# Rotary embedding from PSUM on VectorE, and stabiliser rows loaded in four parts, in a hybrid mLSTM and window-attention layer

## The chip, the cores and the metric

The kernel runs on 1 core of one Trainium2 chip. The metric is the device time of one launch in microseconds (us). The engines are TensorE (PE, with PEld for its weight loads), VectorE (DVE), ScalarE (ACT), GpSimd (POOL) and SyncE (SP), which issues nearly all DMAs.

## The reference

One layer of a diffusion backbone, in float32: 1024 latent tokens and 256 context tokens of width 1024. The tokens are normalised and modulated, and one projection `u = h @ w_in` gives the inputs of two groups of heads:

```
q_m, k_m = silu(dwconv3(qk))          # mLSTM, 4 heads x 128, both directions, stabilised by running maxima
q_a, k_a, v_a                         # window attention, 8 query heads and 2 key heads x 64
y_a = window_attention(rope(q_a) * 64**-0.5, rope(k_a), v_a, k_ctx, v_ctx, sink)
rope: y0 = x0*cos - x1*sin ; y1 = x0*sin + x1*cos      # x0, x1: 16 columns each, twice in a head of 64
x = x + g_a * (concat(y_m, y_a) @ w_out)
x = x + g_f * conv_glu(modulate(rmsnorm(x)))
```

The mLSTM decays are exp(d - m), and the rows of m (the stabilisers) are needed along the free dimension of a tile, the same in all partitions.

## The kernel before

All large products split each operand into a high and a low half that TensorE takes at its fast rate, and sum three products. The work goes in this order:

1. **Norm and shared projection** (to about 78 us of the span). Tokens are normalised, transposed and modulated; `px_mm` projects block c (128 tokens) onto gates, keys and values of the attention, and `px_out(c)` takes the result out of PSUM: VectorE adds the gate biases (L321), ScalarE copies the values into the tile `kv` (L326), which has 3 buffers, and `kv` is stored to DRAM by SP. Keys of latent blocks (c from 2 on) are rotated in between: a ScalarE copy to `kr`, two GpSimd products with the cosine and sine tables (`ta`), a GpSimd subtraction and a GpSimd addition. The blocks 6 and 7 lie in the two banks of one PSUM tile (`pa`), whose slot the first product of `dense` (tile `pp`, L583) takes next. The order of PE, DVE, ACT and POOL is written out by hand here.
2. **Head 0's projection** (`dense(0)`), where a planner orders all engines, and the chain of gate arithmetic (`gate_chain`), which ends with the rows of m in the DRAM tensor `m_d`.
3. **Four mLSTM heads** (about 128 to 376 us). `mlstm(h)` is a generator; each of its 30 steps is followed by products of `dense(h+1)` or, in the last head, of the query projection (`qgen`), so that TensorE has other work. Beside it, `ada_second` streams the rest of `w_ada` in 64 pieces of 256 KB (tile `w2`, 2 buffers: piece i issues the load of piece i+2) and multiplies and adds them on VectorE (L812, L814). At a head's start `ee` (8 blocks, 1 buffer) is loaded from `m_d`, broadcast to all partitions, in one DMA of 1 MB (L641); `mask(b)` adds the triangle on VectorE (L654), `decay(b)` takes the two exponentials on ScalarE (L658), and `first` multiplies with the scores (L714). In the first loop of 9 steps, which carries the backward state (L679, L681), step i does `mask(i-1)`. In the heads 0 to 2 the order of all engines and of SP's DMAs is the program's; in head 3 only PE's is, and the planner orders the others.
4. **Query projection, to about 413 us**: 16 times 24 matmuls into PSUM (`px`, 2 buffers), then the rotation into `z`, the split into `qs` (`qtrans`: ScalarE L865, VectorE L866), a transpose on TensorE (L870) and a store to `q_d`. The transposes of one step are emitted some steps later (`LAG`). Three tiles of `w_out` are multiplied by a gate row, on VectorE, GpSimd and VectorE (`load_wo`, L878).
5. **Attention with the output projection** (to about 600 us), all engines ordered by the planner; then the ConvGLU and the down projection, which take the rest of the span.

Of the kernel before, what the change touches and what calls it, by code (L numbers as in the profile page):

```python
# [8 lines left out]
F32 = mybir.dt.float32  # L9
F32R = mybir.dt.float32r  # L10
BF16 = mybir.dt.bfloat16
AF = mybir.ActivationFunctionType
ALU = mybir.AluOpType
# [4 lines left out]
P = 128  # L18
# [55 lines left out]
def build(tc, I, out, dbg=None):  # L74
# [229 lines left out]

    pxs = {}

    def px_mm(c, kts):
        if c not in pxs:
            if c in (6, 7):

                pxs[c] = pas[-1][:, 512 * (c - 6):512 * (c - 6) + 512]
            else:
                pool, tag = (pl, "l") if c >= 2 else (pd, "d")
                pxs[c] = pool.tile([P, 512], F32, name="px", tag=tag)
        px = pxs[c]
        for kt in kts:
            mm3(px[:, :XW], hsl(0, kt, c), hsl(1, kt, c), wX[0][:, kt, :], wX[1][:, kt, :], kt == K0[0], kt == K1[-1])

    def px_out(c):
        px = pxs.pop(c)  # L320
        V.tensor_tensor(out=gates[:, c, :], in0=px[:, 0:16], in1=rwc("gate_b"), op=ALU.add)  # L321
        kv = xp.tile([P, 2 * P], F32, name="kv", tag="kv", bufs=3)
        if c < NC:
            S.copy(kv[:], px[:, 16:XW])
        else:
            S.copy(kv[:, P:], px[:, 16 + P:XW])  # L326
            kr = xp.tile([P, P], F32, name="kr", tag="kr")
            S.copy(kr[:], px[:, 16:16 + P])  # L328
            ta = xp.tile([P, 2, P], F32, name="ta", tag="ta", bufs=1)
            for i in range(2):  # L330
                G.tensor_tensor(out=ta[:, i].rearrange("p (h e) -> p h e", h=KVH),
                                in0=kr[:].rearrange("p (h e) -> p h e", h=KVH),
                                in1=rope[:, i, c - NC].unsqueeze(1).broadcast_to([P, KVH, ADH]), op=ALU.mult)
            tv = ta[:].rearrange("p i (a s j) -> p i a s j", s=2, j=16)
            kvv = kv[:, :P].rearrange("p (a s j) -> p a s j", s=2, j=16)
            G.tensor_tensor(out=kvv[:, :, 0], in0=tv[:, 0, :, 0], in1=tv[:, 1, :, 1], op=ALU.subtract)
            G.tensor_tensor(out=kvv[:, :, 1], in0=tv[:, 1, :, 0], in1=tv[:, 0, :, 1], op=ALU.add)
        nc.sync.dma_start(kv_d[c], kv[:])

    K0, K1 = (1, 3, 0, 2), (5, 7, 4, 6)  # L340
# [289 lines left out]
    def mlstm(h, kT, qT, va):  # L630
# [7 lines left out]


        ee = tp.tile([P, NL, 2, P], F32, name="ee", tag="ee", bufs=1)  # L640
        nc.sync.dma_start(ee[:], m_d[:].rearrange("(c h) d t -> h c d t", h=H)[h:h + 1, NC:].broadcast_to([P, NL, 2, P]))  # L641
        def tr(c):
            pn = pl.tile([P, 512], F32, name="pn", tag="l")
            T.transpose(pn[:, 0:P], kT[:, c * P:(c + 1) * P], ident[:])
# [8 lines left out]
        def mask(b):  # L653
            V.tensor_tensor(out=ee[:, b], in0=ee[:, b], in1=tri[:], op=ALU.add)  # L654
# [10 lines left out]
        for i, c in enumerate(order[1][:-1]):  # L665
            pn, kwb = ahead.pop(0)
            if i + 2 < NCH - 1:
                ahead.append(tr(order[1][i + 2]))
            elif i + 2 == NCH - 1:
                tr(order[1][i + 2])  # L670
            T.matmul(pn[:, P:P + E1], kwb[:], va[:, c], start=True, stop=True)
            if c == 1:
                nx = tp.tile([P, E1], F32, name="cst", tag="cst")[:]
            elif c == 0:
                nx = cbk[:, NL - 1]
            else:
                nx = cbk[:, c - NC - 1]
            if prev is None:
                V.tensor_copy(nx, pn[:, P:P + E1])  # L679
            else:  # L680
                V.scalar_tensor_tensor(out=nx, in0=prev, scalar=g1(gd, 1, c), in1=pn[:, P:P + E1],  # L681
                                       op0=ALU.mult, op1=ALU.add)
            prev = nx
            if fins and i:
                next(fins[0])
            if i:
                mask(i - 1)
            if i and i % 2 == 0:
                decay(i // 2 - 1)
            if i == TN:  # L690

                S.activation(yv, yv, AF.Tanh, scale=0.5)
                V.scalar_tensor_tensor(out=yv, in0=yv, scalar=1.0, in1=rwc("gain", h * DH, DH).unsqueeze(1)
                                       .broadcast_to([P, NL, DH]), op0=ALU.add, op1=ALU.mult)
            yield
# [48 lines left out]
        for c in range(NC):  # L744
            pn = pl.tile([P, 512], F32, name="pn", tag="l")
            step(c, pn[:, 0:E1])
            if c == 0:
                cfs.clear()
            decay(4 + c)
            yield  # L750
        first(NC)
        tail = None
# [1 line left out]
        for c in range(NC, NCH):  # L754
            if c + 1 < NCH:
                first(c + 1)
            if tail:
                next(tail)
            yield
            if c < NC + 2:  # L760
                decay(6 + c - NC)
            if tail:
                next(tail)
            tail = second(c)
            yield
# [75 lines left out]
    def qproj(i, b):  # L841
# [5 lines left out]
                yield 0.64  # L847
        if i == 0:
            zs.append(pq.tile([P, 2, 2 * P], F32, name="z", tag="p_", bufs=PB, padded_shape=[P, 2, 320]))
        qt = zs[b][:, i]  # L850
        S.activation(qt, px[:, :256], AF.Copy, scale=float(ADH) ** -0.5)  # L851
        ta = xp.tile([P, 2 * P], F32, name="ta3", tag="ta", bufs=1)
        q4 = qt.rearrange("p (h e) -> p h e", h=4)
        rp_ = lambda j: rope[:, j, b].unsqueeze(1).broadcast_to([P, 4, ADH])
        G.tensor_tensor(out=ta[:].rearrange("p (h e) -> p h e", h=4), in0=q4, in1=rp_(1), op=ALU.mult)  # L855
        V.tensor_tensor(out=q4, in0=q4, in1=rp_(0), op=ALU.mult)
        tv = ta[:].rearrange("p (a s j) -> p a s j", s=2, j=16)
        qv = qt.rearrange("p (a s j) -> p a s j", s=2, j=16)
        G.tensor_tensor(out=qv[:, :, 0], in0=qv[:, :, 0], in1=tv[:, :, 1], op=ALU.subtract)
        G.tensor_tensor(out=qv[:, :, 1], in0=qv[:, :, 1], in1=tv[:, :, 0], op=ALU.add)  # L860

    def qtrans(i, b):
        qs = pq.tile([P, 4, 2, ADH], F32R, name="qs", tag="qs", bufs=3)
        qh = zs[b][:, i].rearrange("p (h e) -> p h e", h=4)
        S.copy(qs[:, :, 0], qh)  # L865
        V.tensor_tensor(out=qs[:, :, 1], in0=qh, in1=qs[:, :, 0].bitcast(F32), op=ALU.subtract)  # L866
        yield
        pt = pl.tile([P, 512], F32, name="pt", tag="l")
        for j in range(4):
# [75 lines left out]
    for h in range(H):  # L945
# [20 lines left out]
        with tc.manual_schedule(engines=order_):  # L966
            dn = dense(h + 1, wkq, wvo, *nh) if nh else qgen()
            rate = RATE if nh else RATE3
            for n, _ in enumerate(mlstm(h, *cur)):
# [9 lines left out]
                elif nh and n in (24, 27):  # L979
                    wkq = wnext((n // 27,))  # L980
                    if n == 27 and h + 2 < H:
                        wnext = ahead_load(h + 2, 1)
                elif nh and n % 8 != 7:
                    next(ada, 0)
                debt += rate * (1 + (n == 0))
                while debt > 0:
# [178 lines left out]
            V.tensor_tensor(out=yf[0:64], in0=u[0:64, 0:P], in1=ut[0:64], op=ALU.add)  # L1165
            V.tensor_tensor(out=yf[64:128], in0=u[64:128, P:2 * P], in1=ut[64:128], op=ALU.add)

    wos += [load_wo(k, (G, V)[k % 2], lw, "w4") for k in range(1, 4)]
    w0 = wout_m(0)
    next(w0)  # L1170
    for g in qpend:
# [795 lines left out]
def host_pack(inp):  # L1967
# [55 lines left out]
    inv = (10000.0 ** (-np.arange(16, dtype=np.float32) / 16)).astype(np.float32)  # L2023
    ang = np.stack([(t // 64).astype(np.float32)[:, None] * inv, (t % 64).astype(np.float32)[:, None] * inv], 1)
    tab = np.stack([np.cos(ang), np.sin(ang)], 0).astype(np.float32)
    tab = np.repeat(tab[:, :, :, None, :], 2, 3).reshape(2, NL, P, ADH)
    r["rope"] = np.ascontiguousarray(tab.transpose(2, 0, 1, 3))
    return r

# [17 lines left out]
```

## Time and profile before

| | us |
|---|---|
| median of 3 runs | 1310.68 (1309.24 to 1312.76) |
| profiled execution, its own time | 1308.92 |
| span of its trace | 1306.9 |
| time around the span | 2.0 |
| TensorE busy in the span | 1255.5 |
| VectorE busy | 980.7 |
| ScalarE busy | 635.3 |
| GpSimd busy | 253.1 |

The times of the rows below are from the profiled execution, in us from the start of its span. A busy TensorE is not one at its peak, and a granted clock below 1.00 makes its matmuls longer.

### The profile page before, as it was taken

How to read it: one execution, taken by the hardware profiler on the slowest of the kernel's cores; microseconds unless marked ns; L12 is line 12 of the kernel's file. 1: busy time of each engine (PE TensorE's matmuls, PEld its weight loads, DVE VectorE, ACT ScalarE, POOL GpSimd, SP SyncE). 2: the span in 40 equal slices, each digit the busy share in tenths (PEclk: the TensorE clock that was granted, in tenths of full speed). 3: DMA queues.
4: the chain of work that ended last, by engine and by line, in shares of the span. 5: the costliest groups of instructions: out<-in, count | busy, mean ns of one | idle time of the engine just before them, and what ended most of it. 6: DMA issues, size and time to landing. Idle time of an engine off the chain costs nothing.

```text
span 1306.9 us, 19479 instructions
## 1 busy us (share of the span) xinstructions
PE 1255.5 (96%) x7071; PEld 1068.6 (82%) x7071; DVE 980.7 (75%) x1752; ACT 635.3 (49%) x1295; POOL 253.1 (19%) x252
## 2 busy tenths in 40 slices
PE   6999999999898999999989999999999999999997
PEld 4789998989898777878768788888888888788886
DVE  5754777777665888897898777777777776867887
ACT  6632546464764666776664333333333333434435
POOL 1240000000134223332411222222212222001000
PEclk9999999999998999999989999999999999999999
DMA  9431535362245322211422333322322326975653
GB/s 362 169 117 35 156 116 149 106 174 73 66 144 179 113 66 97 78 69 64 147 97 97 105 105 105 112 99 105 104 97 105 105 105 235 340 283 165 202 199 130
DMA packets 90226, 175.64 MB, mean 134 GB/s; under 512 B 12746, under 2 KB 29330, under 8 KB 90130
## 3 DMA queue, kind: packets, MB, share of 16 engines
q1 hardware_dynamic: 89842, 173.61, 39.7%
q8 instruction: 56, 0.92, 0.3%
q10 hardware_dynamic: 288, 0.79, 0.2%
q14 instruction: 40, 0.33, 0.1%
HBM read 136.04 MB, written 38.33 MB: 133 GB/s over the span
## 4 chain that ended last, share of the span: by engine, by line
PE 53%; DVE 8%; ACT 3%; DMA 2%; issue 2%; POOL 1%; SPq 0%; ACTq 0%; DVEq 0%; POOLq 0%
PE pd L1892 14%; PE pc L1384 8%; PE pa L1384 8%; PE pe L1384 4%; PE pb L1384 4%; PE pd L1384 4%; PE u L1154 2%; PE po L301 2%; PE po L303 2%; PE po L302 1%; DVE nm L1102 1%; PE pt L1131 1%; DMA ar<-act_s 1%; DVE nm L1103 1%; PE pf L1384 0%
## 5 line engine op out<-in xcount | busy, mean ns | idle before, releaser
L1486 ACT CAST wh<-Rb 128x1024 fp32r<-128x1024 f32 (+1 forms) x66 | 59.5, 904 | 144.6 <-PE pd L1384 81.6
L1892 PE MATMUL pd<-dh,al 128*128 128x512 f32 x296 | 115.5, 390 | 0.8 <-DVE al L1258 0.8
L1892 PE MATMUL pd<-dl,ah 128*128 128x512 f32 x296 | 115.4, 390 | 0.0
L1892 PE MATMUL pd<-dh,ah 128*128 128x512 f32 x296 | 115.3, 389 | 0.0
L1384 PE MATMUL pc<-hB,wh 128*128 128x512 f32 x344 | 106.5, 391 | 1.1 <-DVE av L1463 1.1
L1384 PE MATMUL pa<-hB,wh 128*128 128x512 f32 x336 | 103.7, 390 | 0.0
L1274 DVE TENSOR_TENSOR wl<-Rb,wh 128x1024 fp32r<-128x1024 f32 (+1 forms) x66 | 68.9, 1046 | 39.4 <-ACT wh L1486 38.8
L1594 POOL TENSOR_TENSOR tt<-vt,tt 128x512 f32<-128x512 f32 x22 | 29.5, 1341 | 321.5 <-ACT tt L1588 321.5
L583 PE MATMUL pp<-hl,wh 128*128 128x512 f32 x256 | 79.4, 406 | 1.3 <-ACT kr L328 1.3
L1384 PEld LDWEIGHTS pc<-hB,wh 128*128 128x128 f32 x344 | 64.8, 189 | 15.0 <-DVE av L1463 1.6
L301 PE MATMUL pv<-wh,hl 128*128 128x256 f32 x256 | 76.0, 297 | 0.0
L1384 PEld LDWEIGHTS pa<-hB,wh 128*128 128x128 f32 x336 | 63.0, 188 | 13.4 <-ACT sn L1558 0.4
L303 PE MATMUL pv<-wh,hl 128*128 128x256 f32 x256 | 72.4, 283 | 0.0
L302 PE MATMUL pv<-wl,hl 128*128 128x256 f32 x256 | 72.4, 283 | 0.0
L855 POOL TENSOR_TENSOR ta<-z,rope 128x256 f32<-128x256 f32 x16 | 13.4, 838 | 285.4 <-ACT z L851 285.4
L1384 PE MATMUL pc<-hB,wl 128*128 128x512 f32 x172 | 67.0, 389 | 0.0
L1892 PEld LDWEIGHTS pd<-dh,al 128*128 128x128 f32 x296 | 55.6, 188 | 12.9 <-DVE al L1258 1.5
L1384 PE MATMUL pa<-hB,wl 128*128 128x512 f32 x168 | 65.4, 389 | 0.0
L1892 PEld LDWEIGHTS pd<-dl,ah 128*128 128x128 f32 x296 | 55.6, 188 | 11.9 <-DVE dl L1258 0.3
L1892 PEld LDWEIGHTS pd<-dh,ah 128*128 128x128 f32 x296 | 55.6, 188 | 11.5
L1138 ACT CAST ph<-pt 128x512 fp32r<-128x512 f32 (+1 forms) x88 | 45.3, 526 | 21.8 <-PE pt L1131 21.3
L1102 DVE TENSOR_REDUCE nm<-sps 128x1 f32<-128x640 f32 (+1 forms) x64 | 50.0, 783 | 6.3 <-PE sps L1098 5.7
(1078 smaller groups left out, 3836.4 us busy)
## 6 DMA issues: line engine op xcount, KB each, us to landing
w<-in_w_ada_dram SPq DMA_DIRECT2D x64, 256.0 KB, 2.7
br<-in_w_down_dram SPq DMA_DIRECT2D x25, 512.0 KB, 6.3
Ra<-in_w_up_dram SPq DMA_DIRECT2D x22, 512.0 KB, 3.6
Rb<-in_w_up_dram SPq DMA_DIRECT2D x22, 512.0 KB, 3.6
ar<-act_s SPq DMA_DIRECT2D x44, 256.0 KB, 3.1
act_a<-tt SPq DMA_DIRECT2D x33, 256.0 KB, 2.0
act_s<-tt SPq DMA_DIRECT2D x33, 256.0 KB, 2.0
wr<-in_w_h_dram SPq DMA_DIRECT2D x16, 512.0 KB, 4.4
```

The source lines that it names most:

```text
L301: T.matmul(ps, st_hi, mv_hi, start=first, stop=False)
L302: T.matmul(ps, st_hi, mv_lo, start=False, stop=False)
L303: T.matmul(ps, st_lo, mv_hi, start=False, stop=last)
L583: T.matmul(pp[:, 512 * n:512 * n + 512], wkq[sw][:, kt, cs], hl[n][part][:, kt, :], start=kt == 0 and sw + part == 0, stop=kt == KT - 1 an ...
L1102: V.tensor_reduce(out=self.nm[:, j:j + 1], in_=self.sv[j], axis=AX.X, op=ALU.max, negate=True)
L1138: S.copy(self.ph[i][:, :w], self.pt[i][:, :w])
L1154: T.matmul(self.u[:], vv[:, c, self.g], part[i][:, kk * 2 * P:(kk + 1) * 2 * P], start=kb + m == 0, stop=kb == last and m == 1)
L1274: sub = lambda e, o, x, y: e.tensor_tensor(out=o, in0=x, in1=y, op=ALU.subtract)
L1384: T.matmul(ps[:], wt[sw][:, j, ks], hB[part][:, blk, kt, :], start=first and kt == 0 and sw + part == 0, stop=last and kt == 3 and sw == 1 ...
L1486: S.copy(wt[0][:], src)
L1594: G.tensor_tensor(out=self.tt[:, h2_], in0=self.vt[:], in1=self.tt[:, h2_], op=ALU.mult)
L1892: T.matmul(ps[:], ac[sa][:, js], w[sw], start=first and n == 0, stop=last and n == 2, skip_group_check=not fresh)
```

## The change

Four edits. **Rotation**: keys and queries are rotated by three VectorE operations, the two products reading PSUM, the third an addition in place whose second input has each pair of 16-column groups swapped; the sine table on the host gets the sign. The ScalarE copies `kr` and `z` are gone, and the scale of 1/8 goes into the split in `qtrans`. **Rows**: `ee` is loaded in four DMAs of two blocks, one at the head's start and one in each of the steps i = 0, 1, 2; `mask` and `decay` come a step or two later. **Pieces of `w_ada`**: no longer in the steps n = 0 and 1 of a head, but in n = 7 and 23. **`w_out`**: all three gate products on VectorE.

```
+    def rotate(dst, src, nh, b):
+        ta = xp.tile([P, nh * ADH], F32, name="ta", tag="ta", bufs=1)
+        hv = lambda a: a.rearrange("p (h e) -> p h e", h=nh)
+        sv = lambda a: a.rearrange("p (a s j) -> p a s j", s=2, j=16)
+        for i, o in ((1, ta[:]), (0, dst)):
+            V.tensor_tensor(out=hv(o), in0=hv(src), in1=rope[:, i, b].unsqueeze(1).broadcast_to([P, nh, ADH]), op=ALU.mult)
+        V.tensor_tensor(out=sv(dst), in0=sv(dst), in1=sv(ta[:])[:, :, ::-1], op=ALU.add)
...
             S.copy(kv[:, P:], px[:, 16 + P:XW])
-            kr = xp.tile([P, P], F32, name="kr", tag="kr")
-            S.copy(kr[:], px[:, 16:16 + P])
-            ta = xp.tile([P, 2, P], F32, name="ta", tag="ta", bufs=1)
-            for i in range(2):
-                G.tensor_tensor(out=ta[:, i].rearrange("p (h e) -> p h e", h=KVH),
...
-            G.tensor_tensor(out=kvv[:, :, 0], in0=tv[:, 0, :, 0], in1=tv[:, 1, :, 1], op=ALU.subtract)
-            G.tensor_tensor(out=kvv[:, :, 1], in0=tv[:, 1, :, 0], in1=tv[:, 0, :, 1], op=ALU.add)
+            rotate(kv[:, :P], px[:, 16:16 + P], KVH, c - NC)
...
-        nc.sync.dma_start(ee[:], m_d[:].rearrange("(c h) d t -> h c d t", h=H)[h:h + 1, NC:].broadcast_to([P, NL, 2, P]))
+        def ee_load(b):
+            nc.sync.dma_start(ee[:, b:b + 2], m_d[:].rearrange("(c h) d t -> h c d t", h=H)
+                              [h:h + 1, NC + b:NC + b + 2].broadcast_to([P, 2, 2, P]))
+
+        ee_load(0)
...
             prev = nx
+            if i < 3:
+                ee_load(2 * i + 2)
             if fins and i:
                 next(fins[0])
-            if i:
-                mask(i - 1)
-            if i and i % 2 == 0:
-                decay(i // 2 - 1)
+            if i > 1:
+                mask(i - 2)
+            if i in (4, 6, 8):
+                decay(i // 2 - 2)
...
-            decay(4 + c)
+            if c == 0:
+                mask(NL - 1)
+            decay(3 + c)
...
-            if c < NC + 2:
-                decay(6 + c - NC)
+            if c < NC + 3:
+                decay(5 + c - NC)
...
-        qt = zs[b][:, i]
-        S.activation(qt, px[:, :256], AF.Copy, scale=float(ADH) ** -0.5)
-        ta = xp.tile([P, 2 * P], F32, name="ta3", tag="ta", bufs=1)
...
-        G.tensor_tensor(out=ta[:].rearrange("p (h e) -> p h e", h=4), in0=q4, in1=rp_(1), op=ALU.mult)
-        V.tensor_tensor(out=q4, in0=q4, in1=rp_(0), op=ALU.mult)
...
-        G.tensor_tensor(out=qv[:, :, 0], in0=qv[:, :, 0], in1=tv[:, :, 1], op=ALU.subtract)
-        G.tensor_tensor(out=qv[:, :, 1], in0=qv[:, :, 1], in1=tv[:, :, 0], op=ALU.add)
+        rotate(zs[b][:, i], px[:, :256], 4, b)
...
-        S.copy(qs[:, :, 0], qh)
-        V.tensor_tensor(out=qs[:, :, 1], in0=qh, in1=qs[:, :, 0].bitcast(F32), op=ALU.subtract)
+        S.activation(qs[:, :, 0], qh, AF.Copy, scale=float(ADH) ** -0.5)
+        V.scalar_tensor_tensor(out=qs[:, :, 1], in0=qh, scalar=float(ADH) ** -0.5, in1=qs[:, :, 0].bitcast(F32),
+                               op0=ALU.mult, op1=ALU.subtract)
...
-                elif nh and n % 8 != 7:
+                elif nh and n >= 3 and n != 15:
                     next(ada, 0)
...
-    wos += [load_wo(k, (G, V)[k % 2], lw, "w4") for k in range(1, 4)]
+    wos += [load_wo(k, V, lw, "w4") for k in range(1, 4)]
...
-    tab = np.repeat(tab[:, :, :, None, :], 2, 3).reshape(2, NL, P, ADH)
+    tab = np.repeat(tab[:, :, :, None, :], 2, 3)
+    tab[1, :, :, 1] *= -1
+    tab = tab.reshape(2, NL, P, ADH)
```

## Rows read from the trace of the kernel before

**Rows 1.** The page's first part: busy us of each engine in the span, its share, and the number of instructions.

```profile
PE 1255.5 (96%) x7071; PEld 1068.6 (82%) x7071; DVE 980.7 (75%) x1752; ACT 635.3 (49%) x1295; POOL 253.1 (19%) x252
```

**Rows 2.** Busy time of each engine in stretches of the span. Columns: the stretch and its length, then busy us (and instructions) of PE, PEld, DVE, ACT and POOL, the granted clock of TensorE, the DMA share and GB/s.

```profile
62.00:90.00 28.00, 25.39 (x161) 22.86 (x160) 14.52 (x41) 10.56 (x25) 18.28 (x34) 1.00 0.40 113
128.00:200.00 72.00, 72.00 (x518) 67.18 (x517) 49.29 (x115) 36.19 (x109) 0.00 (x0) 1.00 0.46 136
200.00:265.00 65.00, 63.73 (x460) 59.21 (x459) 49.27 (x121) 34.97 (x99) 0.00 (x0) 1.00 0.42 127
330.00:375.00 45.00, 39.64 (x316) 37.85 (x315) 31.45 (x106) 33.70 (x106) 8.78 (x15) 0.96 0.24 72
375.00:425.00 50.00, 45.63 (x360) 42.72 (x358) 29.80 (x60) 25.86 (x62) 23.12 (x36) 0.93 0.62 190
450.00:560.00 110.00, 104.84 (x719) 86.44 (x720) 97.52 (x243) 76.49 (x199) 38.81 (x43) 1.00 0.24 82
```

**Rows 3.** The waits of TensorE between 60 and 450 us: who waited, for whom, us in total, how many times, the longest.

```profile
PE pn L644 <- DVE cst L679: 2.4, 2, 1.2
PE pn L644 <- DVE cbk L681: 2.1, 1, 2.1
PE pn L671 <- ACT kwf L650: 1.6, 3, 1.2
PE pt L870 <- DVE qs L866: 1.5, 3, 0.9
PE pa L303 <- DVE hl L297: 1.3, 2, 0.7
PE pp L583 <- ACT kr L328: 1.3, 1, 1.3
PE pt L870 <- DVE nm L1103: 1.2, 1, 1.2
...
PE pt L870 <- ACT QTo L872: 0.9, 1, 0.9
```

**Rows 4.** The timeline of VectorE in the heads 1, 2 and 3 of the mLSTM: start, length, the instruction, and in brackets the idle time before it and what ended it.

```profile
204.95 0.49 DVE L812 TENSOR_SCALAR acc<-w,scc 128x512 f32<-128x512 f32 x1 [6.83 <-DMA w<-in_w_ada_dram]
205.35 0.28 DVE L679 COPY cst<-pn 128x129 f32<-128x129 f32 x1
...
274.23 0.75 DVE L814 SCALAR_TENSOR_TENSOR acc<-w,scc,acc 128x512 f32<-128x512 f32 x1 [6.50 <-DMA w<-in_w_ada_dram]
...
341.85 0.76 DVE L654 TENSOR_TENSOR ee<-ee,tri 128x256 f32<-128x256 f32 x2 [3.08 <-DMA ee<-m_d]
342.52 0.34 DVE L681 SCALAR_TENSOR_TENSOR cbk<-cbk,gd,pn 128x129 f32<-128x129 f32 x1
```

**Rows 5.** The instructions on the tile `ee`: line, engine, operation, count, shortest, median and longest ns, the first and last start, and the shape; and the time of its loads from issue to landing.

```profile
L654 DVE TENSOR_TENSOR ee<-ee,tri x32: 374/420/428, 139.7 to 348.2; 128x256 f32<-128x256 f32 x32
L714 DVE SCALAR_TENSOR_TENSOR ee<-pe,ee x32: 409/417/425, 158.2 to 368.2; 128x256 f32<-128x256 f32 x32
L641 SPq DMA_DIRECT2D ee<-m_d x4: 366/372/382, 130.3 to 333.7; - x4
...
DMA to landing us min/median/max: 8.1/9.3/9.8
```

**Rows 6.** DMA issues: tile and source, queue, count, KB each, median us from issue to landing.

```profile
w<-in_w_ada_dram SPq DMA_DIRECT2D x64, 256.0 KB, 2.7
```

**Rows 7.** The instructions of the rotation, in the form of rows 5: those on the tile `ta`, the ScalarE copy, and VectorE's product in the last 50 us of the stage.

```profile
L331 POOL TENSOR_TENSOR ta<-kr,rope x16: 454/463/1478, 61.9 to 84.4; 128x128 f32<-128x128 f32 x16
L855 POOL TENSOR_TENSOR ta<-z,rope x16: 728/740/1761, 344.8 to 413.3; 128x256 f32<-128x256 f32 x16
L859 POOL TENSOR_TENSOR z<-z,ta x16: 454/460/578, 347.5 to 414.6; 128x128 f32<-128x128 f32 x16
...
L851 ACT ACTIVATE z<-px x16: 365/377/387, 344.3 to 412.8; 128x256 f32<-128x256 f32 x16
...
L856 DVE TENSOR_TENSOR z<-z,rope x11: 411/425/426, 378.7 to 414.1; 128x256 f32<-128x256 f32 x11
```

**Rows 8.** The timeline of VectorE and ScalarE around the blocks of keys and values.

```profile
61.17 0.17 DVE L321 TENSOR_TENSOR gates<-px,rw 128x16 f32<-128x16 f32 x1
61.38 0.27 ACT L326 COPY kv<-px 128x128 f32<-128x128 f32 x1 [0.84 <-DVE gates L321]
64.24 0.70 DVE L297 TENSOR_TENSOR hl<-ym,hl 128x512 fp32r<-128x512 f32 x1 [2.90 <-POOL ym L292]
...
77.91 0.27 ACT L326 COPY kv<-pa 128x128 f32<-128x128 f32 x1 [5.12 <-DMA kv_d<-kv]
```

**Rows 9.** The timeline of GpSimd and VectorE where GpSimd multiplies a tile of `w_out`.

```profile
398.74 2.39 POOL L878 TENSOR_TENSOR wor<-wor,rga 128x1024 f32<-128x1024 f32 x1
...
399.25 2.16 DVE L866 TENSOR_TENSOR qs<-z,qs 128x256 fp32r<-128x256 f32 x1 [1.09 <-ACT qs L865]
```

**Rows 10.** The stretches of 4 us in which TensorE's granted clock fell, between 300 and 450 us; columns as in rows 2.

```profile
344.00:348.00 4.00, 3.55 (x16) 3.25 (x17) 4.00 (x14) 3.43 (x14) 1.19 (x2) 0.57 0.22 82
416.00:420.00 4.00, 2.98 (x10) 2.04 (x11) 4.00 (x8) 3.56 (x6) 0.00 (x0) 0.51 0.90 247
420.00:424.00 4.00, 4.00 (x19) 3.22 (x18) 1.00 (x6) 0.87 (x3) 1.35 (x2) 0.64 0.75 282
```

**Rows 11.** The instructions of the tile `wor` on VectorE, in the form of rows 5.

```profile
L878 DVE TENSOR_TENSOR wor<-wor,rga x3: 1215/1217/1226, 389.0 to 424.8; 128x1024 f32<-128x1024 f32 x3
```

More of the change, by code (lines that the diff above doesn't have):

```diff
@@ L326, in px_out @@
             S.copy(kv[:, P:], px[:, 16 + P:XW])
-            kr = xp.tile([P, P], F32, name="kr", tag="kr")
-            S.copy(kr[:], px[:, 16:16 + P])
-            ta = xp.tile([P, 2, P], F32, name="ta", tag="ta", bufs=1)
-            for i in range(2):
-                G.tensor_tensor(out=ta[:, i].rearrange("p (h e) -> p h e", h=KVH),
[L332 to L335, printed above, removed]
-            G.tensor_tensor(out=kvv[:, :, 0], in0=tv[:, 0, :, 0], in1=tv[:, 1, :, 1], op=ALU.subtract)
-            G.tensor_tensor(out=kvv[:, :, 1], in0=tv[:, 1, :, 0], in1=tv[:, 0, :, 1], op=ALU.add)
+            rotate(kv[:, :P], px[:, 16:16 + P], KVH, c - NC)
         nc.sync.dma_start(kv_d[c], kv[:])
@@ L849, in qproj @@
             zs.append(pq.tile([P, 2, 2 * P], F32, name="z", tag="p_", bufs=PB, padded_shape=[P, 2, 320]))
-        qt = zs[b][:, i]
-        S.activation(qt, px[:, :256], AF.Copy, scale=float(ADH) ** -0.5)
-        ta = xp.tile([P, 2 * P], F32, name="ta3", tag="ta", bufs=1)
-        q4 = qt.rearrange("p (h e) -> p h e", h=4)
-        rp_ = lambda j: rope[:, j, b].unsqueeze(1).broadcast_to([P, 4, ADH])
-        G.tensor_tensor(out=ta[:].rearrange("p (h e) -> p h e", h=4), in0=q4, in1=rp_(1), op=ALU.mult)
-        V.tensor_tensor(out=q4, in0=q4, in1=rp_(0), op=ALU.mult)
-        tv = ta[:].rearrange("p (a s j) -> p a s j", s=2, j=16)
-        qv = qt.rearrange("p (a s j) -> p a s j", s=2, j=16)
-        G.tensor_tensor(out=qv[:, :, 0], in0=qv[:, :, 0], in1=tv[:, :, 1], op=ALU.subtract)
-        G.tensor_tensor(out=qv[:, :, 1], in0=qv[:, :, 1], in1=tv[:, :, 0], op=ALU.add)
+        rotate(zs[b][:, i], px[:, :256], 4, b)
     def qtrans(i, b):
```

## The prediction

> **What bounds the kernel now.** I read the page's first part, then the busy time by stage, then TensorE's own waits, then the timeline at each wait. The reader should see that TensorE is busy 96% of the span [rows 1], so another engine's work counts only where TensorE waits for it, or where its clock falls. It stands idle 2.6 us among the keys and values (62 to 90 us), not at all in head 0 (128 to 200), 1.3 us in head 1 (200 to 265), but 5.4 and 4.4 us in the two stretches from 330 to 425 us [rows 2]. The list of TensorE's waits names the causes, and most touch the edits: the backward state (L679, L681, 2.4 and 2.1 us), a copy in head 3 (L650), the splits of queries (L866, 1.5), keys and modulated tokens (L328, L297), and the last two query steps (0.9 and 1.2) [rows 3]. The clock falls twice, each time right after such waits: to a mean of 0.57 in 344 to 348 us and of 0.51 and 0.64 in 416 to 424 us, that is to its lower level of 1.2 GHz for part of each [rows 10]. A mean of 0.57 over 4 us costs (1 - 0.57) x 4 = 1.7 us of full-speed work, the second fall 1.96 + 1.44 = 3.4 us.
>
> **The change part by part.**
>
> *Keys.* GpSimd's order puts two modulating products behind the rotation of block 2, and VectorE stands 2.90 us waiting for them [rows 8]; TensorE loses 1.3 us there [rows 3]. With GpSimd free these products can run before, so that I give back all 1.3. The other wait, 1.3 us before `pp`, is for block 7's copies: ScalarE's copy into `kv` stood 5.12 us because an earlier store of `kv` had not landed [rows 8]. The stores now follow a shorter chain, so this wait should shrink, but SP has other loads in front of them; I take half, 0.7. VectorE's price: a 128x256 operation on PSUM takes 417 ns [rows 5] and a 128x16 one 170 [rows 8]; on the line between them 128x128 is about 0.285 us (an estimate). Eight blocks by three are 6.8 us more on an engine busy 14.5 of 28 [rows 2], so 76%. One thing speaks against it. ScalarE's copy starts at 61.38, 40 ns after the gate addition on the same PSUM tile ends (61.17 + 0.17) [rows 8]: the two engines read a tile one after the other. So the rotation must wait for that copy, and VectorE, in order, stands wherever the copy waits for a store; behind it are the next gates, the splits of head 0's weights and the gate chain. If the store lands no earlier than now, `pp` opens after one copy and two products (0.27 + 0.57) and not after two copies (0.54 at most): 0.3 later, with a change of engine up to 0.5, whatever was gained ahead of it. Keys: **2.0 us**, from -0.5 to 2.6. The Trainium skill has this as a rule ("PSUM — Partial Sum Buffer", section "PSUM bank collisions raise a hardware error"): two engines must not read one bank at a time, reads against reads included. By that rule, the trace agrees, the low bound is the case in which a store is late.
>
> *Heads 1 and 2.* VectorE stands 6.83 and 6.50 us for a 256 KB piece of `w_ada` in the step before L679 [rows 4]. Such pieces land in 2.7 us [rows 6]; these were issued behind the 1 MB of `ee`, which takes 8.1 to 9.8 [rows 5]. L679 behind them keeps TensorE from its next slot, 1.2 us each [rows 3]. Now no piece stands in steps 0 and 1, and only 256 KB of rows go first; the pieces of step 3 were issued in the head before. The later parts of `ee` are issued in steps 2 to 4 between pieces, in SP's written order, and each is first read four steps later (about 2 us a step, 30 steps in 65 us [rows 2]), against 2.7 us for a load of that size. SP issues 3 more DMAs of 0.37 us a head [rows 5], on a queue that waits more than it works. The pieces in steps 7 and 23 are 0.75 us of VectorE work each [rows 4], under TensorE's filler products. **2.4 us**, from 0 to 2.4. Head 0 has no idle TensorE [rows 2] and gains nothing. Masks and decays keep count and length; what moves still comes steps ahead of L714, so 0.
>
> *Head 3.* VectorE's first mask waits 3.08 us for the whole of `ee`, L681 stands behind it [rows 4], TensorE waits 2.11 us, then 1.19 us more for a copy that ScalarE does after the delayed exponentials [rows 3], and then runs 4 us at a mean clock of 0.57. A quarter of the load should land in some 3 us and not in 8 to 9, before the first mask now needs it, and each mask is a step later. 2.11 + 1.19 + 1.7 = **5.0 us**; if only half of the waits go and the clock still falls, 1.6. A rule of the Trainium skill speaks against parts ("DMA: Bandwidth & Descriptors", section "Bandwidth": batch transfers to at least 1 MiB). By the rows four loads of 256 KB one after the other are 4 x 2.7 = 10.8 us against 9.3 [rows 5, 6], so the last part comes 1.5 us later than the whole does now, the first 6.6 earlier. By that rule the last masks would be the late ones, which is a rival below.
>
> *Queries.* A step's chain was ScalarE 0.38, GpSimd 0.74, VectorE 0.43, GpSimd 2 x 0.46, then the split [rows 7]; now three VectorE operations of about 0.42 in a row, 1.26 against 2.47 plus four changes of engine. No row has the reversed groups of 16 on VectorE: below, 0.417 as for L714 [rows 5]; above, GpSimd's own price for the strided form against the dense one, 2 x 0.46 against 0.74, which is 1.24 times, so 0.52. I take 0.42, since only strides differ. The one long split, 2.16 us for 0.42, ran beside GpSimd's 2.39 us product on `w_out` [rows 9], which now takes 1.22 on VectorE [rows 11]. So the 1.5 us behind L866 should go (0.6 if the longest, 0.9, stays away and the rest remains gone only in part): **1.5 us**. At the end, 0.9 us waited for a ScalarE copy that stood behind a split waiting for GpSimd, and 1.2 for the last query's chain, which is now more than 1.2 us shorter: **2.1 us**, at least 0.5. The clock's second fall comes right behind; whether it goes I leave open, 0 to 3.4, taking 0, because the fall's work would then partly wait for the splits of `w_out`.
>
> *New cost.* In 375 to 425 us VectorE is busy 29.8 of 50 [rows 2]; 11 query steps [rows 7] x 2 more operations x 0.42 are 9.2, the product on `w_out` 1.2: 40.2 of 50. That hides behind TensorE's 24 matmuls a step, unless a 1.22 us operation stands in front of a rotation whose PSUM buffer is wanted. I charge one, **-1.3 us** with its hand-over; at most three, -3.7; at least 0.
>
> Sum: 2.0 + 2.4 + 5.0 + 1.5 + 2.1 - 1.3 = 11.7 us. The profiled execution took 1308.92, so 1297.2; it lies 1.76 under the median of the runs, so against 1310.68 the forecast is **1299.0**.
>
> **The rivals.**
>
> (a) *The parts arrive late.* The third and fourth quarter, queued behind pieces of `w_ada`, hold the masks of the steps 6 and 8, and with them L681. Then heads 1 and 2 give 0 and head 3 1.6: 2.0 + 1.6 + 1.5 + 2.1 - 1.3 = 5.9, or 1304.8. For it: SP's order and 10.8 against 9.3 us; against it, four steps of time.
>
> (b) *The clock also stays up at the hand-over to attention*: 11.7 + 3.4 = 15.1, or 1295.6. For it: both waits ahead of 416 us are in the edited chain. Against it: the stretch had only 2.98 of 4 us busy [rows 10], and the attention's start has waits of its own.
>
> (c) *VectorE becomes the bound in keys and queries.* Keys -0.5, splits 0.6, the end 0.5, new cost -3.7, heads as above 7.4: 4.3, or 1306.4. It needs more than 0.72 us an operation: (50 - 29.8 - 1.2) / 11 = 1.73, plus the 0.43 it already had, over three.
>
> (d) *Slower.* The attention is ordered by the planner from its own costs, and the edited chain feeds it; VectorE is busy 97.5 of 110 us there [rows 2], more than in any other stage. If the new order puts one VectorE operation in front of each pair's maximum, TensorE waits in each of 34 pair steps. With 0.5 us each it is 17 us, 1316.0; it decides from 11.7 / 34 = 0.34 us a step. Against it: nothing in that stage itself is edited.
>
> **How the numbers follow.** The forecast has 0.50 with its own range of 1294 to 1304, (a) 0.15, (b) 0.15, (c) 0.12, (d) 0.08. This kernel can tell 0.3%, 3.9 us, from no change, so faster means under 1306.8. Of the forecast's half I put 0.03 above that (several terms at their low ends at once), of (a) 0.03, of (c) half: faster 0.47 + 0.12 + 0.15 + 0.06 = 0.80, same 0.12, slower 0.08. All terms at their best make 2.6 + 2.4 + 5.0 + 1.5 + 2.1 + 3.4 = 17.0, or 1293.7. The range runs from 1293 to 1308: it leaves out (d), the worse third of (c) and the edges of (b), under 0.2.
>
> **What would show it.** In the profile after: GpSimd busy under 220 us (253.1 [rows 1] less 16 x 0.463, 16 x 0.74, 32 x 0.46 and 2.4 [rows 7, 9], 36 us, and the small key operations); no wait of `pn` for L679 in the heads 1 and 2; VectorE's first mask of head 3 waiting under 1 us and a clock of 1.00 at 340 to 350 us; `pp` waiting under 1 us; the transposes of queries without a wait for `qs`; rotations of about 0.42 us; the attention as long as before. Wrong I would be if VectorE stands behind a `kv` store while TensorE waits, if masks wait for the third or fourth quarter, or if the stretch after 416 us grows by what the heads gave.

## The result and the profile after

The kernel after takes 1299.05 us (median; 1298.61 to 1300.43), beside 1311.24 us for the kernel before, run on the same chip: a ratio of 0.991, with a 95% interval of 0.9893 to 0.9927. The forecast was 1299.0. Below, a ratio to the kernel before is turned into time by 1311 us.

The profiled execution after took 1300.43 us, 1.4 above its median, while that of before lies 2.3 below the median of these runs. So the two traces differ by 8.3 us of span and not by 12.2, and what stage after stage shows here adds up to 8.3. The page after, its first lines:

```profile
span 1298.6 us, 19413 instructions
PE 1255.1 (97%) x7071; PEld 1069.9 (82%) x7071; DVE 993.2 (76%) x1809; ACT 630.7 (49%) x1271; POOL 208.1 (16%) x171
```

GpSimd fell by 45 us, to the forecast's "under 220"; VectorE took up only 12.5 of them [rows 1]. TensorE's busy time is the same (1255.1 against 1255.5), so what these two traces differ by is its idle time (43.5 against 51.4 us). The clock gave nothing in this pair: between 20 and 700 us its falls cost 10.3 us after and 8.5 before, by the sum that is explained in the last section. Busy time by stage, columns as in [rows 2]:

```profile
62.00:90.00 28.00, 28.00 (x189) 26.10 (x188) 20.76 (x69) 11.21 (x20) 0.00 (x0) 1.00 0.44 137
200.00:265.00 65.00, 64.06 (x469) 60.06 (x469) 50.81 (x124) 34.92 (x101) 0.00 (x0) 1.00 0.44 133
330.00:375.00 45.00, 41.71 (x347) 39.84 (x346) 37.07 (x130) 35.34 (x104) 0.00 (x0) 1.00 0.31 100
375.00:425.00 50.00, 45.85 (x334) 41.75 (x333) 36.52 (x81) 24.53 (x54) 5.07 (x6) 0.93 0.51 164
```

Among keys and values TensorE has no idle time left (2.6 us before). Head 1 still has 0.9 of 1.3, and the stretch from 330 to 375 us, most of it head 3, has 3.3 of 5.4. TensorE's waits after in the heads 1 to 3, from 195 to 366 us (who waited, for whom, us in total, times, the longest; `pn` holds transposed keys and new states, `pj` the products with the states, `pi` those with `ee`):

```profile
PE pj L727 <- DVE ee L719: 1.0, 1, 1.0
PE pi L730 <- DVE ee L719: 0.8, 1, 0.8
PE pn L647 <- DVE cbk L684: 0.8, 2, 0.5
PE pn L647 <- DVE cst L682: 0.6, 1, 0.6
...
PE pn L704 <- DVE ada L809: 0.6, 1, 0.6
```

And from 365 to 430 us, the queries and the hand-over to the attention (`pt` holds transposes, `po` the output projection):

```profile
PE pt L1129 <- POOL p__5055 L1117: 1.3, 1, 1.3
PE pt L1027 <- ACT QTo L870: 0.9, 1, 0.9
PE po L301 <- ACT wo L878: 0.8, 1, 0.8
PE pt L868 <- ACT QTo L870: 0.6, 1, 0.6
```

The waits for the first state of the heads 1 and 2 (L679 before, L682 now) and those of query transposes for `qs` are gone [rows 3]. New ones stand elsewhere: for `ee` and `ada` in the heads 1 and 2 (225 and 288 us), for `ee` in head 3 (355 us), and for GpSimd's product `p` at the hand-over to the attention. The stretches with a lower granted clock, columns as before, with the one that had fallen in head 3:

```profile
344.00:348.00 4.00, 4.00 (x37) 4.00 (x36) 3.97 (x11) 4.00 (x12) 0.00 (x0) 1.00 0.04 10
408.00:412.00 4.00, 4.00 (x13) 3.04 (x12) 2.10 (x6) 2.07 (x7) 0.00 (x0) 0.57 0.94 299
416.00:420.00 4.00, 3.00 (x15) 2.27 (x16) 2.26 (x8) 2.02 (x6) 0.56 (x1) 0.84 0.00 0
420.00:424.00 4.00, 4.00 (x16) 3.16 (x16) 1.43 (x7) 1.12 (x4) 2.75 (x4) 0.73 0.00 0
532.00:536.00 4.00, 4.00 (x24) 3.44 (x23) 3.29 (x10) 1.10 (x3) 1.57 (x2) 0.65 0.00 2
```

Head 3 keeps 2.4 GHz now (0.57 before [rows 10]). At the hand-over 1.7 and 0.6 + 1.1 us are lost, 3.4 as before. In this execution 1.7 more go at 528 to 536 us, behind a wait of 1.2 us that before did not have.

Where the time went, by the starts of the same instructions in the two timelines: the first `pp` comes 2.7 us earlier, the last `pe` of the heads 0, 1, 2 and 3 by 2.8, 3.1, 3.8 and 6.1, the last transpose of queries by 11.0, but the last score product of the attention only by 7.1 and the last matmul of the kernel by 7.7.

### The profile page after: what moved, and what is told of

It reads as the page before. It is cut to its first block, busy times and chain, and to the rows that moved or that the text cites. A ratio compares the mean times of both kernels' runs of the same rounds, so it can differ in the third digit from the quotient of the medians.

```text
span 1298.6 us, 19413 instructions
## 1 busy us (share of the span) xinstructions
PE 1255.1 (97%) x7071; PEld 1069.9 (82%) x7071; DVE 993.2 (76%) x1809; ACT 630.7 (49%) x1271; POOL 208.1 (16%) x171
## 4 chain that ended last, share of the span: by engine, by line
PE 79%; DVE 9%; ACT 4%; DMA 4%; issue 2%; POOL 1%; SPq 0%; ACTq 0%; DVEq 0%; POOLq 0%
PE pd L1890 14%; PE pc L1382 9%; PE pa L1382 9%; PE pp L582 6%; PE pb L1382 4%; PE pe L1382 4%; PE pd L1382 4%; PE u L1152 3%; PE pv L301 2%; PE pv L303 2%; PE pv L302 2%; PE px L303 2%; PE px L301 2%; PE px L302 2%; PE po L301 1%
## 5 line engine op out<-in xcount | busy, mean ns | idle before, releaser
L301 PE MATMUL pv<-wh,hl 128*128 128x256 f32 x256 | 75.9, 296 | 0.0
L303 PE MATMUL pv<-wh,hl 128*128 128x256 f32 x256 | 72.3, 283 | 0.0
L1890 PEld LDWEIGHTS pd<-dh,ah 128*128 128x128 f32 x296 | 55.6, 188 | 11.7 <-ACT ah L1255 0.4
L1382 PE MATMUL pe<-hB,wh 128*128 128x512 f32 x176 | 54.2, 389 | 0.0
```

Source lines behind the costliest of these rows:

```text
L301: T.matmul(ps, st_hi, mv_hi, start=first, stop=False)
L303: T.matmul(ps, st_lo, mv_hi, start=False, stop=last)
L1382: T.matmul(ps[:], wt[sw][:, j, ks], hB[part][:, blk, kt, :], start=first and kt == 0 and sw + part == 0, stop=last and kt == 3 and sw == 1 ...
L1890: T.matmul(ps[:], ac[sa][:, js], w[sw], start=first and n == 0, stop=last and n == 2, skip_group_check=not fresh)
```

## Experiments

Three theories stood at the start. T1: each part's gain stays to the end, and what is lost at the hand-over belongs to the queries' edit. T2: the hand-over takes back whatever comes earlier. T3: the terms of my sum.

**Keys alone (e1_keys).**

The edit in `px_out` and the signed table, without the others:

```diff
-            kr = xp.tile([P, P], F32, name="kr", tag="kr")
-            S.copy(kr[:], px[:, 16:16 + P])
...
+            rotate(kv[:, :P], px[:, 16:16 + P], KVH, c - NC)
```

> The kernel before with the rotation of the keys alone moved to VectorE; queries, rows and the piece steps stay as before (its old query rotation adds where it subtracted, since the table carries the sign). Theory T1 (each part's gain stays to the end; the loss at the hand-over belongs to the queries' edit): the first pp opens 2.7 us earlier, as in the kernel after, and the whole is 2 to 3 us faster, ratio about 0.998. Rival T2 (whatever arrives earlier at the hand-over to attention is taken back there, because something off TensorE sets the start of the attention): pp 2.7 us earlier, the first score product of the attention at most 1 us earlier, the whole within 1 us. Rival T3 (my prediction's term): 2.0 us.

Measured: 1307.13 us, ratio 0.9963 (0.9948 to 0.9977), so 4.9 us, from 3.0 to 6.8. The first `pp` is 2.8 us earlier. T2 falls; T3's 2.0 is too small, and T1's "2 to 3" is at the interval's edge. The profiled execution itself is only 0.7 us shorter in span than that of before: its clock losses sum to 10.3 us against 8.5, with one between 28 and 32 us, in nothing that the edit touches.

**Queries alone (e2_queries).**

The edits in `qproj` and `qtrans` and the signed table, without the others:

```diff
-        S.activation(qt, px[:, :256], AF.Copy, scale=float(ADH) ** -0.5)
...
+        rotate(zs[b][:, i], px[:, :256], 4, b)
```

> The kernel before with the rotation of the queries alone moved to VectorE, with the scaling by the square root moved into the split; the products on w_out stay half on GpSimd; keys, rows and piece steps as before. T1: between the last product of head 3 and the last transpose of queries 4 to 5 us less, of which the hand-over and the attention take 3 to 4 back, so that the whole gains 1 to 2 us. T2: the last transpose of queries 4 to 5 us earlier, the whole within 1 us. T3 (my prediction's terms): 3.6 less 1.3, so 2.3 us faster, with the products on w_out still on GpSimd rather 1.5.

Measured: 1306.36 us, ratio 0.9957 (0.9943 to 0.9972), 5.6 us, from 3.7 to 7.5: more than any theory. TensorE's waits from 365 to 430 us:

```profile
PE pt L1130 <- POOL p__5067 L1118: 1.3, 1, 1.3
PE pt L1130 <- POOL p__5063 L1118: 1.0, 1, 1.0
PE pt L1028 <- ACT QTo L871: 0.9, 1, 0.9
...
```

No transpose waits for `qs`, though GpSimd still multiplies `w_out` there (2.49 us at 397.88). Idle TensorE from 365 to 440 us is 4.3 us, 6.6 before. In the trace the last transpose is 4.7 us earlier and the last score product 2.8.

**Rows and piece steps (e3_rows).**

The edits in `mlstm` and in the loop over its steps; keys, queries and the products on `w_out` as before:

```diff
+            if i < 3:
+                ee_load(2 * i + 2)
...
-                elif nh and n % 8 != 7:
+                elif nh and n >= 3 and n != 15:
```

> The kernel before with the rows of the stabilisers in four parts, masks and decays a step later, and the pieces of w_ada in their new steps; keys and queries rotated as before, products on w_out as before. T1: the three later heads gain what the two profiles differ by there, 0.3 + 0.7 + 2.3 = 3.3 us, and keep it: ratio 0.9975. T2: the heads' end 3.3 us earlier, the whole within 1 us. T3 (my prediction's terms): 2.4 + 5.0 = 7.4 us, ratio 0.994.

Measured: 1306.14 us, ratio 0.9963 (0.9948 to 0.9979), 4.9 us, from 2.8 to 6.8. T3's 7.4 is outside, T2 falls again. The three parts alone make 4.9 + 5.6 + 4.9 = 15.4, with all together 11.8 (9.6 to 14.0): with these intervals that is neither shown to add nor not to. TensorE's waits in the heads 1 and 2:

```profile
PE pi L731 <- DVE ee L720: 1.5, 1, 1.5
PE pn L705 <- DVE ada L810: 0.5, 1, 0.5
```

The two waits of 1.2 us [rows 3] are gone, and others of 1.5 us (head 1) and 0.5 us (head 2) are there. So I took the two edits apart.

**Steps alone (e5_steps) and parts alone (e6_parts).**

The first has only the second hunk of the edit above, the second only `ee_load` with the masks and decays a step later:

```diff
-                elif nh and n % 8 != 7:
+                elif nh and n >= 3 and n != 15:
```

```diff
+            if i < 3:
+                ee_load(2 * i + 2)
...
-                mask(i - 1)
+                mask(i - 2)
```

> The kernel before with one edit of the rows' part: the pieces of w_ada in their new steps (none in the steps 0 to 2 and 15), the rows still loaded as one 1 MB transfer, masks and decays where they were. The whole rows' part gave 4.8 us (ratio 0.9963). Theory S (heads 1 and 2 wait because VectorE stands behind a piece that is queued behind the rows): most of the gain of the heads 1 and 2 is here, their two waits for L679 (1.2 us each) go, head 3 keeps its waits of 2.1 and 1.2 us; 2 to 2.5 us faster. Rival Q (the size of the rows' transfer is what holds the pieces, wherever they stand): VectorE waits for a piece as long as before, gain under 0.5 us.

> The kernel before with the other edit of the rows' part: rows in four parts, masks and decays a step later, and the pieces of w_ada in their old steps. Theory S: head 3's waits of 2.11 and 1.19 us shrink as in the kernel after, and its clock stays up, while the heads 1 and 2 keep a wait; 2.5 to 3 us faster. Rival Q: the waits for L679 in the heads 1 and 2 shorten too, since a piece then stands behind 256 KB and not behind 1 MB, and the edit alone gives the 4.8 us.

Measured: steps alone 1312.23 us, ratio 1.0005 (0.9996 to 1.0015); parts alone 1303.53 us, ratio 0.9937 (0.9924 to 0.9949), 8.3 us, from 6.7 to 10.0. The parts alone gave more than both edits together (0.9963, whose interval just touches theirs); theory S falls, since its two waits for L679 went and no time was gained, and rival Q, that a piece behind 256 KB does not wait long, holds. TensorE's waits from 195 to 366 us with steps alone, and VectorE's timeline at the third:

```profile
PE pn L644 <- DVE cbk L681: 2.7, 1, 2.7
...
PE pi L725 <- DVE ee L714: 1.1, 1, 1.1
...
```

```profile
229.24 0.75 DVE L814 SCALAR_TENSOR_TENSOR acc<-w,scc,acc 128x512 f32<-128x512 f32 x1 [1.35 <-DMA w<-in_w_ada_dram]
229.91 0.42 DVE L714 SCALAR_TENSOR_TENSOR ee<-pe,ee 128x256 f32<-128x256 f32 x1
```

And with parts alone, the same view:

```profile
PE pn L675 <- ACT kwf L654: 0.8, 2, 0.6
PE pn L648 <- DVE cbk L685: 0.7, 2, 0.4
PE pi L731 <- ACT nm L734: 0.6, 1, 0.6
PE pn L648 <- DVE cst L683: 0.4, 1, 0.4
...
```

All of these are in head 3. Idle TensorE between the ends of the heads 0 and 2, from the timelines: 2.7 us before, 2.2 with the steps alone, 0 with the parts alone, 2.2 with both. The new steps take the piece out of the place where it held L679 and put one in front of L714: the steps 7 and 23 had been free, and a piece of 256 KB in nearly every step leaves a load of 2.7 us [rows 6] no step to catch up in (30 steps in 65 us). With whole rows that trade gives nothing; with rows in parts it is a loss. Part of this loss is clock: by the granted clock that is on record for each run, (1 - clock) x span is 5.5 us on average with the parts alone and 8.4 with both edits.

**Old steps in the kernel after (e9_old_steps).**

From here on the edits are to the kernel after:

```diff
-                elif nh and n >= 3 and n != 15:
+                elif nh and n % 8 != 7:
```

> The kernel after with one edit undone: the pieces of w_ada back in their old steps (none in the steps 7, 15 and 23), the rows still in four parts. Theory U (the new steps lose what separates the rows' whole edit, 0.9963, from the parts alone, 0.9937: with the skipped steps 7 and 23 gone, pieces of 2.7 us follow each other in steps of some 2.2 us and VectorE stands for one right before L719): 3 us faster than the kernel after, near 1296, and the wait of pi for L719 in head 1 gone. Rival V (the parts alone were fast because the rest of the kernel was the old one; with keys and queries rotated on VectorE the steps make no difference): within 1 us of the kernel after.

Measured: 1296.33 us, ratio 0.9877 (0.9864 to 0.9891), just clear of the kernel after's interval, 2.7 us under its median (by the two ratios the difference is 4.3). This is what theory U said, in size and place: the end of head 2 comes 2.2 us earlier than in the kernel after, with no idle TensorE left in the heads 1 and 2 (1.5 us in the kernel after). Its waits from 195 to 366 us, all of them in head 3:

```profile
PE pj L727 <- DVE ee L719: 0.8, 1, 0.8
...
PE pn L647 <- DVE cst L682: 0.5, 1, 0.5
...
```

**Products on `w_out` back on GpSimd (e4_wo_pool).**

```diff
-    wos += [load_wo(k, V, lw, "w4") for k in range(1, 4)]
+    wos += [load_wo(k, (G, V)[k % 2], lw, "w4") for k in range(1, 4)]
```

> The kernel after, with the products on w_out for the second and fourth block of rows given back to GpSimd as in the kernel before. If the GpSimd product and the 2.16 us split beside it were worth what my prediction charged: 0 to 1.5 us slower than the kernel after (1299 to 1300.5). If the product on VectorE stands in front of rotations and costs there: up to 1.3 us faster than the kernel after (1298).

Measured: 1299.91 us, ratio 0.9905 (0.9887 to 0.9923): not to be told from the kernel after. This edit gains and costs nothing that can be measured.

**A rotation made dearer (e7_double).**

```diff
-        for i, o in ((1, ta[:]), (0, dst)):
+        for i, o in ((1, ta[:]),) * (1 + (nh == 4)) + ((0, dst),):
```

> The kernel after with the first product of each query rotation done twice on VectorE, so 16 more operations of 0.42 us, 11 of them behind head 3. If VectorE has the slack that my prediction gave it (40.2 of 50 us busy): under 1 us slower than the kernel after. If it is the bound there (the rival of VectorE as the bound): up to 11 x 0.42 = 4.6 us slower, with the query transposes waiting for qs again.

Measured: 1299.54 us, ratio 0.9904 (0.9891 to 0.9918), not to be told from the kernel after. VectorE's busy time, the third figure behind the length, went from 36.5 to 40.8 us in this stretch:

```profile
375.00:425.00 50.00, 46.03 (x347) 42.07 (x346) 40.81 (x96) 24.11 (x55) 4.08 (x6) 0.97 0.52 162
```

Another 4.3 us of VectorE hide as well, as far as these intervals can tell; one transpose waits 0.6 us for `qs` (383 us). VectorE is not the bound there.

**Masks of head 3 on GpSimd (e8_mask_pool), and with the old steps (e11_both).**

```diff
-            V.tensor_tensor(out=ee[:, b], in0=ee[:, b], in1=tri[:], op=ALU.add)
+            (G if h == H - 1 else V).tensor_tensor(out=ee[:, b], in0=ee[:, b], in1=tri[:], op=ALU.add)
```

> The kernel after with the eight masks of head 3 on GpSimd, which does nothing else there, so that VectorE's state updates no longer stand behind a mask that waits for a part of the rows. Theory M (what is left of head 3's term, 0.6 + 0.5 us of waits for the state, comes from the masks being ahead of the state in VectorE's order): about 1 us faster than the kernel after, the waits of pn for L682 and L684 gone. Rival: they are held by TensorE's and ScalarE's own chain, so no change, or 0.5 us slower if GpSimd's masks come late for L719.

> The kernel after with the pieces of w_ada back in their old steps and the masks of head 3 on GpSimd. If the two gains add: 3 us from the steps by theory U and 0.5 to 1.5 from the masks, near 1295; by the rival V 1298.5.

Measured: 1298.52 us, ratio 0.9899 (0.9886 to 0.9913), and with the old steps 1297.33 us, ratio 0.9888 (0.9875 to 0.9902): neither is to be told from the same kernel with the masks on VectorE. In the first trace the last `pe` of head 3 comes 1.6 us earlier, but a wait for the state is still there. GpSimd's masks, and VectorE's work beside them:

```profile
333.98 4.53 POOL L657 TENSOR_TENSOR ee<-ee,tri 128x256 f32<-128x256 f32 x6 [274.27 <-DMA row_d<-arw]
336.31 2.35 DVE L781 SCALAR_TENSOR_TENSOR ym<-hid,hss,ym 128x128 f32<-128x128 f32 x3
338.58 0.34 DVE L684 SCALAR_TENSOR_TENSOR cbk<-cbk,gd,pn 128x129 f32<-128x129 f32 x1
```

Three products that took 0.87 us together in the kernel after take 2.35 here, L684 stands behind them, and TensorE waits 1.1 us for it, as long as for two states together in the kernel after (0.6 + 0.5).

**Products on `w_out` inside the attention on VectorE (e10_wo47).**

```diff
-                        wos.append(load_wo(kt, G, wop))
+                        wos.append(load_wo(kt, V, wop))
```

> The kernel after with the products on w_out for the last four blocks of rows, which run inside the attention, on VectorE and not on GpSimd. Theory W (a GpSimd product of 2.4 us stretches a VectorE operation beside it, as the 2.22 us one at 526 us, and TensorE loses 1.2 us and clock): 1 to 3 us faster than the kernel after, the wait at 528 us gone. Rival: VectorE is the busiest engine beside TensorE there, so 4 x 1.22 us more on it costs what the stretch gave, within 1 us or slower.

Measured: 1303.35 us, ratio 0.9921 (0.9905 to 0.9937); the span of its trace is 4.6 us longer than that of the kernel after, but by the ratios the difference is 1.4 us and the intervals overlap. What it was to cure, in the kernel after:

```profile
525.95 2.37 POOL L876 TENSOR_TENSOR wor<-wor,rga 128x1024 f32<-128x1024 f32 x1 [3.79 <-DMA wor<-in_w_out_dram]
526.12 2.22 DVE L1113 TENSOR_TENSOR ss<-ss,sk 128x2 f32<-128x2 f32 x1
```

and what came in its place, VectorE's timeline here:

```profile
503.41 1.22 DVE L876 TENSOR_TENSOR wor<-wor,rga 128x1024 f32<-128x1024 f32 x1
504.54 1.22 DVE L879 TENSOR_TENSOR wol<-wor,woh 128x1024 fp32r<-128x1024 f32 x1
505.68 0.82 DVE L1100 TENSOR_REDUCE nm<-sps 128x1 f32<-128x640 f32 x1
506.41 1.21 DVE L879 TENSOR_TENSOR wol<-wor,woh 128x1024 fp32r<-128x1024 f32 x1
```

`pl_` comes behind them at 507.61, and TensorE waits 2.4 us for it. Theory W's wait at 528 us is gone, but nothing was gained, and the trace shows the rival's mechanism: at this place in the attention, other than among queries, VectorE had no room for its 1.2 us operations.

**First pair of the attention on VectorE, with the old steps (e12_first_pair).**

```diff
-                G.tensor_scalar(out=self.p[j][:, w], ...
+                (V if self.b + self.h0 == 0 else G).tensor_scalar(out=self.p[j][:, w], ...
```

> The kernel after with the pieces of w_ada in their old steps (1296.3 in the run before this) and, new, the two normalising products of the attention's first pair on VectorE and not on GpSimd, where the second took 1.65 us beside VectorE's split of w_out and TensorE waited 1.3 us for it. Theory X (GpSimd's stretched product is what TensorE waits for, and the clock falls behind that wait): 1.3 us faster, up to 3 with the clock, near 1294. Rival Y (VectorE has the split in front of them in its order, so they end no earlier): within 1 us of 1296.3, the wait of about 1.3 us now for VectorE.

Measured: 1293.4 us, ratio 0.9871 (0.9854 to 0.9888), the fastest kernel here. By the ratios it is not to be told from the old steps alone (0.9877, a difference of 0.8 us), so the time does not decide between X and Y. The two traces differ by 4.3 us of span, and in them Y has the mechanism: both products have ended at 413.0 us, those of GpSimd at 413.1. What differs is what TensorE does until then, and the clock. At 412 to 416 us, the kernel with the old steps and then this one:

```profile
412.00:416.00 4.00, 2.53 (x11) 1.81 (x11) 2.53 (x7) 2.03 (x6) 1.10 (x1) 0.83 0.00 0
```

```profile
412.00:416.00 4.00, 3.56 (x16) 2.59 (x17) 2.98 (x10) 2.03 (x6) 0.44 (x1) 1.00 0.00 0
```

The planner made the order of TensorE's work anew and put matmuls of `w_out` (L301 to L303) where the wait of 1.3 us stood (0.9 us are now waited for VectorE's split of `w_out`), and the fall to 0.83 and 0.74 that followed is gone from this trace, 1.7 of the 4.3 us.

## Why the prediction was right, and where its steps were not

The time is right (1299.05 against 1299.0) and inside the range; the sum is right because errors of both signs cancel, which is luck: alone, the keys and the queries gave more than their terms, the rows less.

*Keys, forecast 2.0.* The mechanism is right and the size low. All 2.6 us of idle time went, at the upper bound, and the whole is worth 3.0 to 6.8. The step that failed is "I take half, 0.7": the store did hold a copy and VectorE behind it, just as feared, in the timelines of ScalarE and VectorE:

```profile
74.63 0.27 ACT L335 COPY kv<-pa 128x128 f32<-128x128 f32 x1 [3.41 <-DMA kv_d<-kv]
74.93 0.29 DVE L313 TENSOR_TENSOR ta<-pa,rope 128x128 f32<-128x128 f32 x1 [2.77 <-ACT kv L335]
```

but TensorE was still at head 0's projection of the context keys (`pc`), and `pp` opened without a wait. VectorE starts 30 ns after the copy ends: the order of two readers of one PSUM tile that the prediction read from [rows 8] is seen here too. What of the 4.9 lies beyond 2.6 no wait shows; it stays open.

*Heads 1 and 2, forecast 2.4.* The cause was right, the remedy was misread. I let the new steps remove the waits and the parts do no harm. The parts alone remove all 2.7 us; the new steps bring 1.5 back in the kernel after. The step that failed is the one on the pieces in the steps 7 and 23, which took them as 0.75 us of VectorE work each and no more: I priced the work and not the load in front of it, against 2.7 us a load and 2.2 us a step that stood in my own rows. In the kernel after, VectorE's timeline in head 1, just before TensorE's wait of 0.8 us for L719:

```profile
225.05 0.75 DVE L821 SCALAR_TENSOR_TENSOR acc<-w,scc,acc 128x512 f32<-128x512 f32 x1 [0.85 <-DMA w<-in_w_ada_dram]
225.72 0.42 DVE L719 SCALAR_TENSOR_TENSOR ee<-pe,ee 128x256 f32<-128x256 f32 x1
```

*Head 3, forecast 5.0.* The clock's 1.7 us came, and were a low price: in the four traces with whole rows head 3 lost 1.7, 3.4, 3.4 and 3.4 us of clock (before, e1, e2, e5), in the ten with parts nothing but for 1.7 in e11_both. The step that failed is that both waits would go: those for states and copies (L644 and L671 before, L647 and L674 now) fell from 3.7 to 2.0 us in all, one of 1.0 us came, and the idle time in head 3 fell by 1.2 (4.5 to 3.3). The loads after, from issue to landing (KB each, median us):

```profile
w<-in_w_ada_dram SPq DMA_DIRECT2D x64, 256.0 KB, 2.7
ee<-m_d SPq DMA_DIRECT2D x16, 256.0 KB, 4.7
```

and the rotations after, in the form of [rows 5]:

```profile
L313 DVE TENSOR_TENSOR ta<-px,rope x22: 282/417/425, 62.3 to 402.4; 128x256 f32<-128x256 f32 x16, 128x128 f32<-128x128 f32 x6
L314 DVE TENSOR_TENSOR z<-z,ta x16: 414/418/426, 339.8 to 403.4; 128x256 f32<-128x256 f32 x16
```

A part takes 4.7 us (3.5 to 7.3), not the 2.7 of a piece of the same size. In head 3 the planner issues the four within 2.1 us, and they land after 3.8, 5.1, 6.3 and 7.3. The planner puts masks 0 to 3 ahead of the first two state updates, and VectorE waits 1.5 and 0.7 us for parts (1.5, where I had said under 1). Still, a first part after 3.8 beats the whole, which took 8.1 in head 3 [rows 5]. The new wait, at 355 us, is for L719, in front of which VectorE does, among others, a split of weights (1.23 us) and a query's rotation and split (4 operations of 0.41). The forecast charged such work only from 375 us on; that the rotation is what costs this 1.0 us is not shown, since e2_queries has the rotation and not the wait. The Trainium skill's rule ("DMA: Bandwidth & Descriptors", section "Bandwidth") to batch to 1 MiB would have kept the load whole. Here the measurement decides: four transfers of 256 KB were worth 0.63% (e6_parts), and in its trace TensorE has no idle time left in the heads 1 and 2, at DMA shares of 0.44 and 0.36.

*Queries, forecast 3.6 less 1.3.* The durations are as taken: 0.42 us, reversed groups included. Behind head 3 the new cost does not show, and neither do the further products of e7_double, within intervals of some 2 us. The splits' waits are gone, but not through the product on `w_out` (e2_queries and e4_wo_pool): the chain of GpSimd alone did it. Of the 2.1 us at the end only 0.6 went, since waits for two ScalarE copies (0.6 and 0.9) now stand there, and the wait of 0.8 at 371 us for `nm`, which I had not priced, went too. Queries alone are worth 3.7 to 7.5.

*The rivals.* (a) is seen in small: VectorE waits for parts, in head 3 and for the early ones. (b) did not come in the profiled executions: 3.4 us of clock loss at the hand-over before and after. How often it comes is open: in the traces of e7_double and e8_mask_pool the hand-over lost 1.7, and the profiled execution is the one of the kernel after's four that lost most clock (last section). (c) falls with e7_double for the queries, and for the keys with TensorE's 28.00 busy of 28 us. (d) named the right place, with a wrong size. Every edit makes the planner order the attention anew: from the first to the last score product it took 182.2 to 186.4 us in the traces of kernels that leave the attention itself alone, 184.1 before and 186.4 after. The forecast "as long as before" was wrong by 2.3 us, 0.07 a pair step and not 0.34; the one wait at 528 us is 1.2 us, and the clock's fall behind it costs 1.7.

## What to carry to other kernels

When a wait is caused by a load queued behind a larger one, shrink the larger one first, and move the consumer only if its loads keep their slack: compare the load's time with the time of a step. Test each edit of a bundle alone, since one of these cost some 3 us that the others hid. Where an order is planned, every edit upstream draws a new order downstream, and its spread belongs in the range.

## What the runs showed of the hardware

VectorE and GpSimd held each other up where both worked in SBUF. The small VectorE sum of 128x2 took 2.22 us beside GpSimd's product of 2.37, and both ended within 20 ns of each other (528.34 and 528.32); the median of its kind is 0.16. At the hand-over of the kernel after both stretched:

```profile
414.25 0.69 POOL L1117 TENSOR_SCALAR p__5051<-p__5051,ss 128x512 f32<-128x512 f32 x1 [353.86 <-DVE ss L1114]
414.51 1.50 DVE L879 TENSOR_TENSOR wo<-wor,wo 128x1024 fp32r<-128x1024 f32 x1
414.91 1.65 POOL L1117 TENSOR_SCALAR p__5055<-p__5055,ss 128x512 f32<-128x512 f32 x1
```

VectorE's operation, 1.2 us elsewhere, took 1.5 with the first product beside its start, and GpSimd's second product, 0.7 elsewhere, ended 0.55 after VectorE was done. The Trainium skill ("SBUF — State Buffer", section "SBUF: two separate sides") has it as a lock held for a whole instruction when VectorE reads two SBUF inputs beside a GpSimd operation that reads SBUF; these traces agree, and by it a small operation can be held as long as a large one lasts.

TensorE's clock losses between 20 and 700 us, summed as (1 - granted clock) x 4 over the stretches of 4 us, came out between 3.4 and 10.3 us in the traces here, and differ between kernels that do not differ in the stretch of the fall. Those in head 3, at the hand-over and at 528 us stood right behind waits of TensorE; the reverse does not hold, since a wait of 1.4 us at 532 us in e6_parts was followed by no fall. One fall, 1.7 or 3.4 us, is as large as most terms summed here. Each run's mean granted clock is on record too: (1 - clock) x span is 11.7, 10.4, 5.2 and 6.5 us in the four runs of the kernel after, the profiled one first, so one trace is not enough to price a fall.
